# Attention probabilities: dividing on ScalarE and turning by TensorE transposes, in place of one product with a diagonal of 1/sum

## The chip, the cores and the metric

The kernel runs on one core of a Trainium2 chip. The metric is the device time of one execution in microseconds (us), as the median of a few runs. A core has TensorE (PE: matrix products; its weight loads are listed apart as PEld), VectorE (DVE), ScalarE (ACT), GpSimd (POOL) and SyncE (SP, which issues the transfers here). They run side by side and wait for each other by semaphores. TensorE reads from on-chip memory and writes into eight accumulation banks, which the other engines empty.

## The reference, cut to what matters

A decoder trunk of two layers on 512 positions of width 1024. A layer is a feed-forward block, a mixing block and a second feed-forward block, each behind an RMS norm that is modulated by a vector c. The mixing block runs a causal pooling mixer beside latent attention with four heads. In the attention, for each block of 128 queries:

```python
s = (q_nope @ k_nope.T + q_rope @ k_rope.T) * SOFTMAX_SCALE
s = where(qpos >= kpos, s, -inf)
p = softmax(s, axis=-1)      # exp(s - max) / sum
o = p @ v
```

All is in 32-bit floats. The change touches the division by the sum and the way from p (queries on the 128 partitions) to its transpose (keys on the partitions), which the product with v needs.

## The kernel before, in words

Weights come from memory in blocks of up to 128x1024. For each, ScalarE rounds a copy (`hi`, L313) and VectorE takes the rest (`lo`, L316); a product is then three products of rounded values (`mm3`, L324): hi with hi, lo with hi, hi with lo. The values between the stages are split in the same way when they leave their bank (`split_ps`, L507). A product whose operands are plain 32-bit floats is two pairs of weight load and matmul in the trace.

Every instruction is written out in Python in program order, and the framework sorts them into the queues of the engines. A running sum `clock` (L256) books a duration for every product, and functions put off by `later` run at the next `tick` after their booked time; in the attention these are squares and statistics for the norm of the block that follows.

The attention of a layer is eight jobs (L1017): two halves of the queries, four heads each. Job 0 to 3 belong to the first half (query blocks 0 and 1, with 128 and 256 keys), job 4 to 7 to the second (blocks 2 and 3, with 384 and 512 keys). Three functions work on a job:

- `scores`, L1021: per query block the score products and a mask product into one bank (`os`), the negated row maximum on VectorE (L1039, L1040), and one ScalarE instruction that writes exp and leaves its row sum in `sm` (L1042). After both blocks VectorE takes 1/sum (L1046), and builds `dg`, two 128x128 diagonals with 1/sum on them (L1048, `sdg` in the trace).
- `transposes`, L1052: for each pair of a query block and a key block the product of that 128x128 piece of exp with the diagonal of its query block. The piece is the weight, the diagonal streams past it, and the result is turned and divided at once. There are three such products in a job of the first half and seven in one of the second: 40 a layer, 80 in all. Three or four lie side by side in a bank (`t` in the trace), which is then split into `pth` and `ptl`.
- `values`, L1079: the products with v (`opv`), split into `yh` and `yl`.

The loop at L1108 issues the scores of job i, then the transposes of job i-2, then the values of job i-3. Between them stand query projections for heads 2 and 3 (`nope`) and, from step 7 on, output products of the first half (`out_a`, `oo` in the trace). After the last job come the output products of the second half, and then the first products of the feed-forward block (`fg`).

The exp of a job lies in a buffer of the tag `raw`, five of which are shared with the weights that arrive. `dg` has two buffers of its own.

Of the kernel before, what the change touches and what calls it, by code (L numbers as in the profile page):

```python
# [11 lines left out]
F32 = mybir.dt.float32  # L12
# [3 lines left out]
AF = mybir.ActivationFunctionType  # L16
ALU = mybir.AluOpType
AX = mybir.AxisListType

P = 128  # L20
# [62 lines left out]
def trunk(ctx: ExitStack, tc: tile.TileContext, xT, c, pos, vec, cst, ada, wgu, wd, wmix, out):  # L83
    nc = tc.nc
    V, A, G, T = nc.vector, nc.scalar, nc.gpsimd, nc.tensor
# [5 lines left out]
    tmp = ctx.enter_context(tc.tile_pool(name="tmp", bufs=2))  # L91
# [5 lines left out]
    def nm(s):  # L97
        uid[0] += 1
        return f"{s}_{uid[0]}"

    def bank(s="b"):
        return ps.tile([P, S], F32, tag="bank", name=nm(s))
# [35 lines left out]
    ident = const.tile([P, P], F32, name="ident")  # L138
# [117 lines left out]
    clock = [0.0]  # L256
# [5 lines left out]
    def tick():  # L262
        while hooks:
            h = min(hooks, key=lambda e: e[:2])
            if h[0] > clock[0]:
                return
            hooks.remove(h)
            h[2]()

    def mm(o, w, m, start, stop):  # L270
        n = m.shape[-1]
        per = 4 if w.dtype == F32 or (w.dtype == F32R and n < 256) else 1
        clock[0] += per * (n / 2400.0) + 0.0136
        T.matmul(o, w, m, start=start, stop=stop)  # L274
# [30 lines left out]
    def prep(upto, lo_eng=None):  # L305
        while nxt[0] <= min(upto, len(units) - 1):
            key, src, w = units[nxt[0]]
            if nxt[0] not in loaded:
                load(nxt[0])
            raw = loaded.pop(nxt[0])  # L310
            hi = wp.tile([P, 1024], F32R, tag="hi", name=nm("hi"), bufs=NW)
            lo = wp.tile([P, 1024], F32R, tag="lo", name=nm("lo"), bufs=NW)
            A.activation(hi[:, :w], raw[:, :w], AF.Copy)  # L313
            pool = key[0] == "m" and key[2] in POOL_LO
            eng = lo_eng or (G if pool else V)
            eng.tensor_tensor(lo[:, :w], raw[:, :w], hi[:, :w].bitcast(F32), op=ALU.subtract)  # L316
            split[key] = (hi, lo)
            nxt[0] += 1

    def weights(key, ahead=AHEAD):  # L320
        prep(order[key] + ahead)
        return split.pop(key)

    def mm3(blocks, before_hi=None, before_lo=None):  # L324


        n = len(blocks)
        for k, items in enumerate(blocks):
            if before_hi:
                before_hi(k)  # L330
            for o, wh, wl, ah, al in items:
                mm(o, wh, ah, k == 0, False)
            for o, wh, wl, ah, al in items:
                mm(o, wl, ah, False, False)
            tick()
        for k, items in enumerate(blocks):
            if before_lo:
                before_lo(k)
            for o, wh, wl, ah, al in items:
                mm(o, wh, al, False, k == n - 1)  # L340
            tick()
# [165 lines left out]
    def split_ps(o, ts=slice(0, S), sc=None, into=None):  # L507

        hi, lo = into if into is not None else (atile("sh"), atile("sl"))
        if sc is None:  # L510
            A.activation(hi[:, ts], o, AF.Copy)
            V.tensor_tensor(lo[:, ts], o, hi[:, ts].bitcast(F32), op=ALU.subtract)
        else:
            A.activation(hi[:, ts], o, AF.Copy, scale=sc)
            V.scalar_tensor_tensor(lo[:, ts], o, sc, hi[:, ts].bitcast(F32), op0=ALU.mult, op1=ALU.subtract)
        return hi, lo
# [103 lines left out]
    def ffn(l, s, nrm, n_first, steps, end):  # L620
        f = 2 * l + (s == 2)
        c0 = 0
        for h, nf in enumerate(PARTS):
# [24 lines left out]
            if h == 0:  # L648
                keys = [("gu", f, cc, j) for cc in range(n_first) for j in range(2)]
                if isinstance(nrm, Opening):  # L650
                    keys.append(("gu", f, n_first, 0))
                    for ts, os_ in nrm.products(keys):
                        for cc in range(n_first):
                            evac(cc, os_[2 * cc], os_[2 * cc + 1], ts)
                        w = weights(("gu", f, n_first, 1))
                        ou = bank("ou")
                        mm3([[(ou, w[0][:, k * P:(k + 1) * P], w[1][:, k * P:(k + 1) * P], nrm.hh[k], nrm.hl[k])]
                             for k in range(KD)])
                        evac(n_first, os_[-1], ou, ts)
                    n_first += 1  # L660
                else:
                    sc = {}
                    ws = [weights(k, 0) for k in keys]
                    prep(order[keys[-1]] + 4)
                    for ts, os_ in nrm.products(ws):
                        for cc in range(n_first):
                            for o, key in zip(os_[2 * cc:2 * cc + 2], keys[2 * cc:2 * cc + 2]):
                                if ts.start == 0:
                                    sc[key] = nrm.shift(o)
                            evac_first(cc, nrm, os_[2 * cc:2 * cc + 2], [sc[k] for k in keys[2 * cc:2 * cc + 2]], ts)  # L670
                done = n_first
# [149 lines left out]
    def mixer(l, nrm, end):  # L821
# [111 lines left out]
        for h in range(NH):  # L933
            o = bank("okn")
# [22 lines left out]
        for t in range(4):  # L957
            o = bank("ov")
# [10 lines left out]
        for u in range(2):  # L969
            o = bank("oqr")  # L970
# [47 lines left out]
        probs, pts = {}, {}  # L1018
        ya = [(atile("yh"), atile("yl")) for _ in range(0)]

        def scores(job):  # L1021
            half, h = job
            p = wp.tile([P, 1024], F32, tag="raw", name=nm("p"), bufs=NRAW)
            sm = small.tile([P, 2], F32, name=nm("sm"), tag="sm", bufs=4)
            parts = []
            c = 0
            for i in (2 * half, 2 * half + 1):
                n = (i + 1) * P
                nn = max(n, 256)
                qs = slice(i * P, (i + 1) * P)  # L1030
                o = bank("os")
                mm(o[:, :nn], qh[h][0][:, qs], kn[h][0][:, :nn], True, False)
                mm(o[:, :nn], qh[h][1][:, qs], kn[h][0][:, :nn], False, False)
                mm(o[:, :nn], qh[h][0][:, qs], kn[h][1][:, :nn], False, False)
                mm(o[:, :nn], qr[h][:, qs], krh[:, :nn], False, False)
                mm(o[:, :nn], qr[h][:, qs], krl[:, :nn], False, False)
                mm(o[:, qs], identb, negb, False, True)
                m = small.tile([P, 1], F32, name=nm("m"), tag="m", bufs=6)
                V.tensor_reduce(m, o[:, :n], axis=AX.X, op=ALU.max, negate=True)  # L1039
                V.tensor_tensor(m, m, qsc[:, i:i + 1], op=ALU.mult)  # L1040
                pp = p[:, c:c + n]
                A.activation(pp, o[:, :n], AF.Exp, bias=m, scale=qsc[:, i:i + 1], accum_out=sm[:, i % 2:i % 2 + 1])  # L1042
                parts.append(pp)
                c += n
                tick()
            V.reciprocal(sm, sm)  # L1046
            dg = tmp.tile([P, 2, P], F32, name=nm("sdg"), tag="xa", bufs=2)
            V.tensor_tensor(dg, ident.unsqueeze(1).to_broadcast([P, 2, P]),  # L1048
                            sm.unsqueeze(2).to_broadcast([P, 2, P]), op=ALU.mult)
            probs[job] = parts, dg  # L1050

        def transposes(job):  # L1052
            half, h = job
            parts, dg = probs.pop(job)
            hi = wp.tile([P, 1024], F32R, tag="hi", name=nm("pth"), bufs=NW)
            lo = wp.tile([P, 1024], F32R, tag="lo", name=nm("ptl"), bufs=NW)
            for z in (hi, lo):
                G.memset(z[:, 0:P].bitcast(F32), 0.0)
            nj = 2 * half + 2
            last = nj - 1  # L1060
            b0 = bank("t0")

            def tr(dst, i, j):
                mm(dst, parts[i][:, j * P:(j + 1) * P], dg[:, i, :], True, True)

            tr(b0[:, P:2 * P], 1, last)
            tr(b0[:, 2 * P:3 * P], 0, 0)
            tr(b0[:, 3 * P:], 1, 0)
            split_ps(b0[:, P:], slice(P, 512), into=(hi, lo))
            if half:  # L1070
                b1 = bank("t1")
                for j in (1, 2):
                    for i in range(2):
                        tr(b1[:, ((j - 1) * 2 + i) * P:((j - 1) * 2 + i + 1) * P], i, j)
                split_ps(b1, slice(512, 1024), into=(hi, lo))
            tick()
            pts[job] = (hi, lo)
# [142 lines left out]
```

## Time and profile before

| | |
|---|---|
| median of 3 runs | 1812.14 us (1811.38 to 1812.93) |
| the profiled execution | 1813.12 us |
| its span, first to last instruction | 1811.3 us |
| TensorE busy | 1794.9 us, 99% of the span |
| VectorE busy | 1029.7 us, 57% |
| ScalarE busy | 607.2 us, 34% |
| GpSimd busy | 105.2 us, 6% |

The profiled execution is 1.0 us above the median, and 1.8 us of it lie outside the span. The attention stands twice in the span, at about 490 to 536 us and at about 1380 to 1423 us. Successive matmuls overlap in the trace, so the duration of one is longer than what it adds to the chain; what it adds is read from the chain of waits, which follows the work that ended last and gives each piece only its own stretch.

### The profile page before, as it was taken

The numbers are of one execution on the slowest core, as the hardware profiler recorded it, in microseconds if no ns is written. First come the engines' busy times: TensorE is split into PE (matmuls) and PEld (weight loads), VectorE is DVE, ScalarE is ACT, GpSimd is POOL, SyncE is SP. The second block draws the span as 40 slices with busy tenths as digits, with TensorE's granted clock in tenths as the row PEclk, the third lists the DMA queues.
The fourth block names the chain that finished last, engine by engine and source line by source line (L and its number), as shares of the span: only waits on it lengthen the run. The fifth ranks groups of instructions, "written<-read, shape, count | busy, mean of one in ns | idle before, by whom it ended". The sixth has DMA issues, their size and how long they took to land.

```text
span 1811.3 us, 21867 instructions
## 1 busy us (share of the span) xinstructions
PE 1794.9 (99%) x8623; PEld 1505.3 (83%) x8623; DVE 1029.7 (57%) x1591; ACT 607.2 (34%) x906; POOL 105.2 (6%) x206
## 2 busy tenths in 40 slices
PE   7999999999999999999999999999999999999998
PEld 4888888888898888888888888888888988888888
DVE  8675645577878544534676555445787754333333
ACT  3322222344465222223342222223554632221232
POOL 2000000105000000000001000000141000000002
PEclk9999999999999999999999999999999999999999
DMA  8566635633133544534436455443220323233311
GB/s 306 191 220 209 204 126 194 197 100 96 36 100 105 168 147 155 163 118 139 159 111 220 162 196 198 140 139 117 62 88 24 105 82 128 84 104 104 94 47 47
DMA packets 69594, 243.75 MB, mean 135 GB/s; under 512 B 7794, under 2 KB 8946, under 8 KB 69492
## 3 DMA queue, kind: packets, MB, share of 16 engines
q1 hardware_dynamic: 69056, 241.99, 40.8%
q8 instruction: 67, 1.10, 0.3%
q10 hardware_dynamic: 436, 0.38, 0.1%
q14 instruction: 35, 0.29, 0.1%
HBM read 240.24 MB, written 2.10 MB: 134 GB/s over the span
## 4 chain that ended last, share of the span: by engine, by line
PE 98%; DVE 1%; issue 0%; DMA 0%; ACT 0%; POOL 0%; DVEq 0%; ACTq 0%
PE od L274 27%; PE ou L274 25%; PE og L274 24%; PE fg L274 5%; PE oo L274 5%; PE oz L274 5%; PE os L274 2%; PE t L274 1%; PE opv L274 1%; PE oqn L274 1%; PE ov L274 1%; PE okn L274 1%; PE st L274 0%; PE oqr L274 0%; PE rb L274 0%; PE warm L565 0%
## 5 line engine op out<-in xcount | busy, mean ns | idle before, releaser
L313 ACT ACTIVATE hi<-raw 128x1024 fp32r<-128x1024 f32 (+1 forms) x320 | 325.5, 1029 | 377.9 <-PE od L274 211.4
L316 DVE TENSOR_TENSOR lo<-raw,hi 128x1024 fp32r<-128x1024 f32 (+1 forms) x310 | 365.0, 1193 | 52.5 <-ACT hi L313 52.1
L633 DVE TENSOR_TENSOR sg<-sg,ou 128x512 f32<-128x512 f32 x82 | 56.4, 688 | 451.7 <-ACT sg L632 451.7
L274 PE MATMUL od<-gh,hi 128*128 128x512 f32 (+1 forms) x736 | 277.3, 380 | 0.0
L274 PE MATMUL od<-gh,lo 128*128 128x512 f32 (+1 forms) x736 | 277.2, 380 | 0.0
L274 PE MATMUL ou<-hh,hi 128*128 128x512 f32 x656 | 255.2, 389 | 0.0
L274 PE MATMUL ou<-hh,lo 128*128 128x512 f32 x656 | 255.2, 389 | 0.0
L274 PE MATMUL og<-hh,hi 128*128 128x512 f32 x648 | 252.1, 389 | 0.0
L274 PE MATMUL og<-hh,lo 128*128 128x512 f32 x648 | 252.1, 389 | 0.0
L632 ACT ACTIVATE sg<-og 128x512 f32<-128x512 f32 x81 | 48.4, 598 | 607.0 <-PE og L274 607.0
L274 PE MATMUL og<-al,hi 128*128 128x512 f32 x504 | 196.1, 389 | 0.0
L274 PE MATMUL ou<-al,hi 128*128 128x512 f32 x504 | 196.1, 389 | 0.0
L202 DVE SCALAR_TENSOR_TENSOR junk<-ada,c_sb 128x1024 bf16<-128x1024 f32 x144 | 175.3, 1220 | 12.4 <-DMA ada<-in_ada 12.4
L274 PE MATMUL od<-gl,hi 128*128 128x512 f32 (+1 forms) x736 | 176.4, 380 | 0.0
L274 PEld LDWEIGHTS od<-gh,hi 128*128 128x128 f32 x736 | 138.4, 188 | 27.8 <-ACT gh L634 1.2
L693 DVE SCALAR_TENSOR_TENSOR x<-od,mod,x 128x512 f32<-128x512 f32 (+1 forms) x100 | 72.9, 729 | 154.3 <-PE od L274 153.9
L274 PEld LDWEIGHTS od<-gh,lo 128*128 128x128 f32 x736 | 138.4, 188 | 25.9
L274 PEld LDWEIGHTS od<-gl,hi 128*128 128x128 f32 x736 | 134.4, 188 | 26.4
L274 PEld LDWEIGHTS ou<-hh,lo 128*128 128x128 f32 x656 | 123.1, 188 | 25.6
L274 PEld LDWEIGHTS ou<-hh,hi 128*128 128x128 f32 x656 | 123.1, 188 | 25.4
L274 PEld LDWEIGHTS og<-hh,lo 128*128 128x128 f32 x648 | 121.6, 188 | 25.3
L274 PEld LDWEIGHTS og<-hh,hi 128*128 128x128 f32 x648 | 121.6, 188 | 25.2
(249 smaller groups left out, 2318.5 us busy)
## 6 DMA issues: line engine op xcount, KB each, us to landing
raw<-in_wgu SPq DMA_DIRECT2D x176, 512.0 KB, 3.5
ada<-in_ada SPq DMA_DIRECT2D x144, 512.0 KB, 4.4
raw<-in_wd SPq DMA_DIRECT2D x64, 512.0 KB, 4.0
raw<-in_wmix SPq DMA_DIRECT2D x40, 512.0 KB, 3.4
raw<-in_wd SPq DMA_DIRECT2D x32, 384.0 KB, 3.4
raw<-in_wmix SPq DMA_DIRECT2D x6, 384.0 KB, 3.6
x<-in_xT SPq DMA_DIRECT2D x4, 512.0 KB, 5.1
out<-fo SPq DMA_DIRECT2D x7, 256.0 KB, 2.2
```

The lines of the kernel that those rows point to most:

```text
L202: V.scalar_tensor_tensor(junk, w, 1.0, c_sb, op0=ALU.mult, op1=ALU.mult, accum_out=dst)
L274: T.matmul(o, w, m, start=start, stop=stop)
L313: A.activation(hi[:, :w], raw[:, :w], AF.Copy)
L316: eng.tensor_tensor(lo[:, :w], raw[:, :w], hi[:, :w].bitcast(F32), op=ALU.subtract)
L632: A.activation(sg, og, AF.Silu)
L633: V.tensor_tensor(sg, sg, ou, op=ALU.mult)
L693: V.scalar_tensor_tensor(x[d][:, ts], o, gt[:, d:d + 1], x[d][:, ts], op0=ALU.mult, op1=ALU.add)
```

## The change

VectorE no longer builds the diagonals. ScalarE multiplies each of the two blocks of exp by its column of 1/sum, in place, with one copy instruction per block (two a job, 128 and 256 columns wide in the first half, 384 and 512 in the second). The 80 products with a diagonal become 80 transposes of TensorE with the identity, and the running clock books 0.113 us for each, where it booked 4 x 128 / 2400 + 0.0136 = 0.227 us.

```diff
+    def turn(o, m):
+
+        clock[0] += 0.113
+        T.transpose(o, m, ident)
...
             V.reciprocal(sm, sm)
-            dg = tmp.tile([P, 2, P], F32, name=nm("sdg"), tag="xa", bufs=2)
-            V.tensor_tensor(dg, ident.unsqueeze(1).to_broadcast([P, 2, P]),
-                            sm.unsqueeze(2).to_broadcast([P, 2, P]), op=ALU.mult)
-            probs[job] = parts, dg
+            for i, pp in enumerate(parts):
+                A.activation(pp, pp, AF.Copy, scale=sm[:, i:i + 1])
+            probs[job] = parts
 
         def transposes(job):
             half, h = job
-            parts, dg = probs.pop(job)
+            parts = probs.pop(job)
...
             def tr(dst, i, j):
-                mm(dst, parts[i][:, j * P:(j + 1) * P], dg[:, i, :], True, True)
+                turn(dst, parts[i][:, j * P:(j + 1) * P])
```

## Rows read from the trace of the kernel before

**Rows 1.** The page: busy times, TensorE's granted clock in 40 slices, chain by engine.

```profile
PE 1794.9 (99%) x8623; PEld 1505.3 (83%) x8623; DVE 1029.7 (57%) x1591; ACT 607.2 (34%) x906; POOL 105.2 (6%) x206
...
PEclk9999999999999999999999999999999999999999
...
PE 98%; DVE 1%; issue 0%; DMA 0%; ACT 0%; POOL 0%; DVEq 0%; ACTq 0%
```

**Rows 2.** Chain of waits by line, 485 to 550 us, then 1385 to 1440 us.

```profile
by line: PE oo L274 39.6%; PE os L274 22.2%; PE t L274 14.2%; PE opv L274 13.4%; PE oqn L274 10.8%; issue 0.1%
...
by line: PE oo L274 41.9%; PE os L274 19.3%; PE t L274 16.7%; PE opv L274 15.9%; PE fg L274 6.3%; issue 0.1%
```

**Rows 3.** Chain of waits in order of time, first layer: start, length, what.

```profile
497.43 1.38 PE os L274 x12
498.81 0.72 PE t L274 x6
...
505.30 0.72 PE opv L274 x6
...
511.91 1.62 PE t L274 x14
...
516.47 4.36 PE oo L274 x36
520.83 1.56 PE t L274 x14
...
531.15 1.56 PE t L274 x14
532.71 3.00 PE opv L274 x24
```

**Rows 4.** Groups of instructions: the products with the diagonal, and its making.

```profile
L274 PE MATMUL t<-sdg,p 128*128 128x128 f32 x160 | 21.3, 278 | 0.0
...
L274 PEld LDWEIGHTS t<-sdg,p 128*128 128x128 f32 x160 | 19.5, 192 | 0.0
...
L1048 DVE TENSOR_TENSOR sdg<-ident,sm 128x256 f32<-128x256 f32 x16 | 6.7, 420 | 0.5
```

**Rows 5.** Chain of waits elsewhere: one-column products, and the turns at the end.

```profile
415.04 0.79 PE st L274 x8
...
1800.42 1.79 PE tr L274 x16
```

**Rows 6.** Groups of instructions: ScalarE copies with a factor per partition.

```profile
L514 ACT ACTIVATE yph<-op,vec_sb 128x512 fp32r<-128x512 f32 x8 | 5.5, 726 | 0.0
...
L749 ACT ACTIVATE fo<-x,vec_sb 128x256 f32<-128x256 f32 x8 | 3.4, 497 | 0.0
```

**Rows 7.** Stretches of 8 us: length, then busy time of PE, PEld, DVE, ACT, POOL.

```profile
496.00:504.00 8.00, 8.00 (x59) 7.27 (x58) 6.17 (x20) 5.02 (x16) 1.31 (x8) 1.00 0.01 2
504.00:512.00 8.00, 8.00 (x54) 6.62 (x53) 6.17 (x20) 4.36 (x12) 2.33 (x11) 1.00 0.19 66
512.00:520.00 8.00, 8.00 (x63) 7.44 (x62) 5.80 (x15) 5.17 (x14) 1.27 (x8) 1.00 0.20 66
```

**Rows 8.** Timeline of ScalarE in the first layer's attention.

```profile
497.47 0.60 ACT L511 ACTIVATE qh<-oqn 128x512 fp32r<-128x512 f32 x1 [0.38 <-PE oqn L274]
...
506.37 0.78 ACT L1042 ACTIVATE p<-os,m,qsc 128x512 f32<-128x512 f32 x1
507.03 0.21 ACT L1042 ACTIVATION_READ_ACCUMULATOR p<-os,m,qsc 128x1 f32 x1
...
533.26 0.58 ACT L511 ACTIVATE pth<-t 128x512 fp32r<-128x512 f32 x1
```

**Rows 9.** Timeline of VectorE in the first layer's attention.

```profile
507.48 0.15 DVE L1046 RECIPROCAL sm<-sm 128x2 f32<-128x2 f32 x1
...
522.84 0.42 DVE L1048 TENSOR_TENSOR sdg<-ident,sm 128x256 f32<-128x256 f32 x1
...
533.87 0.69 DVE L512 TENSOR_TENSOR ptl<-t,pth 128x512 fp32r<-128x512 f32 x1
```

## The prediction

> **What bounds the kernel now.** I read the page first. TensorE is busy for 99% of the span and holds 98% of the chain that ended last; every slice shows a granted clock of 0.9 or more, the upper level of 2.4 GHz [rows 1]. So time is won or lost only where TensorE's own stretch shrinks or where something makes it wait. Next came the chain cut to the two attention stretches: all of it is TensorE, "issue" is 0.1%, and the products with the diagonal (tile t) hold 14.2% of 65 us in the first layer and 16.7% of 55 us in the second [rows 2]. That is 9.2 us a layer, 18.4 us in all, and over 80 products 0.230 us each. The chain in order of time agrees: 0.72 us for the three of an early job, 1.56 to 1.62 us for the seven of a late one [rows 3]. The group of these products has 160 pairs, so each is two pairs of weight load and matmul [rows 4]. Last I read ScalarE and VectorE in the same stretch, because the change moves work between them: both have room, ScalarE is busy 4.4 to 5.2 of 8 us [rows 7].
>
> **The change part by part.**
>
> *The diagonals* (16 x 0.42 = 6.7 us of VectorE [rows 4]) go. VectorE is not on the chain there, so this is worth nothing by itself; the cover is TensorE at 8.00 of 8 us in each of these stretches [rows 7]. One thing gets earlier: the diagonal of job 7 is made at 522.84, once job 5's buffer is free; its job was ready some 4 us sooner. It was not late for its use at 531.15 [rows 3, 9], so nothing is won.
>
> *The 80 transposes.* No transpose of this kind stands in the trace. The nearest rows from above: half of the present product, one pair that streams the diagonal, costs 1.56 / 14 = 0.111 to 0.72 / 6 = 0.120 us [rows 3]; the turns at the end of the kernel, also two pairs each with 32-bit operands, cost 1.79 / 16 = 0.112 a pair [rows 5]. From below, if a transpose is one pair: products with a single streamed column are the weight load alone, 0.79 / 8 = 0.099 us for the same 128x128 of 32-bit values [rows 5]. And the mask product, one pass of 128 narrow columns with a narrow weight, costs (1.38 - 10 x 0.12) / 2 = 0.09 us, with 0.12 for each of the ten 256-column products, as in opv [rows 3]. These lie close together. I take 0.107 us, between the load alone (0.099) and half of the present product (0.115), since the weight is the same piece of exp and has to be loaded at least once. Then 80 x (0.230 - 0.107) = 9.8 us leave TensorE's stretch; with 0.115 it is 9.2, with 0.099 it is 10.5. The other bound is that it stays two pairs: 0.
>
> *The 16 + 16 copies on ScalarE.* A copy with a factor per partition takes 0.497 us for 256 columns and 0.726 for 512 [rows 6]; by their slope about 0.38 for 128 and 0.61 for 384. A first-half job gets 0.88 us, a second-half job 1.34 us, a layer 8.9 us. ScalarE works in order, and the copies wait for 1/sum: the second exp's sum is read by 507.24 and the reciprocal ends at 507.63 [rows 8, 9], so up to 0.4 us of standing still unless another instruction is put between. Queued behind the copies are the next jobs' exp, pth, yh and the query splits qh. From 496 to 520 us ScalarE is busy 5.02 + 4.36 + 5.17 = 14.6 of 24 us [rows 7]. Added are jobs 1 to 7, 3 x 0.88 + 4 x 1.34 = 8.0 us, and seven waits of some 0.2 us: about 24.0 us. TensorE's own work there loses 19 transposes x 0.123 = 2.3 us, so 21.7 us. ScalarE is then short by up to 2.3 us by the last scores, less if neighbouring instructions overlap as they do now. What hides this is the lag of two steps in the loop: job 4's exp is complete at 507.24 and its turn starts at 511.91, 4.7 us later; behind the last scores stand 4.36 us of oo and then no exp at all [rows 3, 8]. If that cover were gone, 2.3 us a layer would show.
>
> Two places have less cover. At the head, qh of head 3 starts at 497.47 [rows 8] just after job 1's exp, and the scores that need it follow at once on the early turns; copies put ahead of it cost up to 1 us. At the tail, values of job 7 follow the last turn with only values of job 6 between: the turn ends 0.86 us earlier, while the second eviction (pth at 533.26, ptl to 534.56 [rows 8, 9]) may not move, and the 24 products there already take 3.00 us where 24 x 0.12 = 2.88 would do [rows 3]. That gives back 0 to 0.9 us. I take 0.3 us for the head and 0.4 for the tail in each layer: 1.4 us. The range of this term is 0 to 3.5 us.
>
> *The clock of the planner* books 40 x 0.114 = 4.6 us less a layer. It only shifts where squares and statistics are written between the products; their distance to what they wait for stays the same. Nothing. No transfer is added or moved past another, and the exp buffers come free with the turns, sooner than before. Nothing either.
>
> *Sum:* 9.8 - 1.4 = 8.4 us. The profiled execution would go from 1813.1 to 1804.7 us (span 1802.9), and the median, 1.0 us below it, from 1812.1 to **1803.7 us**.
>
> **The rivals.**
>
> *Two pairs remain.* If 32-bit data is turned in two passes, as the present product works, TensorE saves nothing and the copies stay hidden behind an unshortened stretch: 1811.5 to 1813 us. For it: every plain 32-bit product in the trace comes in two pairs [rows 4, 5]. Against: that is how two factors are multiplied, and a transpose multiplies nothing. 0.10.
>
> *A turn does not overlap with its neighbours.* Now each matmul is recorded with 278 ns but adds only 111 to 120 [rows 3, 4], since the next starts before it ends. If transposes could not overlap, each would cost 0.278 us, 80 x (0.278 - 0.230) = 3.8 us more: 1815.9. It decides from 0.230 us upwards; if only the first and last of a job's run stood clear, 32 x 0.16 = 5.1 us of the gain would go. For it: no row shows one. Against: matmuls with different operand types follow each other without such a gap (the mask product's 0.09). 0.04. The Trainium skill ("TensorE: Matmul & The Clock Gate", Part 4: PE-mode transpose) speaks for this side: it gives about 275 ns for a transpose inside a kernel, as an estimate 80 x 0.045 = 3.6 us more, and says that such transposes don't count as busy for the clock. The trace has 278 ns for products that cost 111 to 120, so a duration of that size need not be a price.
>
> *ScalarE paces the attention.* Place: 496 to 520 us of the first layer and its like in the second. If the scores wait for banks that exp frees late, all the copies and waits show, 8.9 + 8 x 0.2 = 10.5 us a layer at most, 21 - 9.8 = 11 us slower, 1823. It ends slower than before once 4.9 us a layer show; by the sum above 2.3 us are there to show. 0.04 for slower; 0.07 for a part of it, 3 to 8 us given back in all and 1806.5 to 1810.
>
> *A turn is cheaper still.* A product of 256 columns costs 0.12 us with its load hidden [rows 3], so 128 columns with a hidden load would be 0.06: 80 x 0.17 = 13.6 us, 1798.5 to 1800. Against it: 0.099 for the load alone. 0.03. The Trainium skill ("TensorE: Matmul & The Clock Gate", Terms) calls the transpose mode four times faster for 32-bit data; by that the estimate is 0.230 / 4 = 0.058 us and a gain of 13.8 us. No row here shows it.
>
> **How the numbers follow.** The forecast has 0.72, with its own range from 9.2 - 3.5 to 10.5 us, 1801.7 to 1806.5. The rivals hold 0.10, 0.04, 0.04 + 0.07 and 0.03. A measurement of this kernel tells a difference of about 0.2% (3.6 us) from none. Faster by more: 0.72 + 0.03 + 0.05 of the part-paced case = 0.80. Within it: 0.10 + 0.02 = 0.12. Slower: 0.08. The range from 1800.0 to 1811.0 takes in the forecast, the part-paced case and the cheaper edge of two pairs.
>
> **What would show it.** One load and one matmul per turn, 80 instead of 160, and pieces of t in the chain of about 0.33 us and 0.75 us instead of 0.72 and 1.56. TensorE at 8.00 of 8 us throughout the attention, with ScalarE near 7 of 8 between 496 and 520. The clock still at the upper level. The forecast is wrong if t keeps two pairs, if the chain shows ScalarE (L1042, L511 or the new copies) before os, opv or t, or if the last values wait for ptl by more than 1 us a layer.

## The result, and the profile after

| | before | after |
|---|---|---|
| median | 1812.41 us (4 runs, 1811.38 to 1812.93) | 1802.83 us (4 runs, 1802.53 to 1803.62) |
| ratio | | 0.9945 (0.9933 to 0.9958) |
| profiled execution | 1813.12 us | 1803.62 us |
| its span | 1811.3 us | 1801.8 us |
| TensorE busy | 1794.9 us | 1786.1 us |
| VectorE busy | 1029.7 us | 1023.2 us |
| ScalarE busy | 607.2 us | 621.1 us |

The change makes the kernel 9.6 us faster, 0.55%. The forecast was 1803.7 us, with 1801.7 to 1806.5 as its own range. The page of the changed kernel, in the lines that answer to [rows 1]:

```profile
PE 1786.1 (99%) x8543; PEld 1496.0 (83%) x8543; DVE 1023.2 (57%) x1575; ACT 621.1 (34%) x938; POOL 103.2 (6%) x206
...
PEclk9999999999999999999999999999999999999999
...
PE 98%; DVE 0%; DMA 0%; ACT 0%; issue 0%; DVEq 0%; ACTq 0%; SPq 0%
```

TensorE still holds the chain, at the same clock, with 80 matmuls fewer. The chain by line, 485 to 550 us and 1375 to 1440 us, where [rows 2] had 14.2% of 65 us and 16.7% of 55 us for t:

```profile
by line: PE oo L274 39.6%; PE os L274 22.2%; PE opv L274 13.6%; PE oqn L274 12.1%; PE t L327 6.8%; PE fg L274 5.9%; issue 0.1%
...
by line: PE oo L274 35.4%; PE os L274 20.1%; PE fg L274 16.2%; PE opv L274 13.6%; PE t L327 6.8%; PE oqn L274 5.8%; PE rb L274 1.4%; PE st L274 1.2%; issue 0.1%
```

That is 4.4 us in each layer, where 9.2 stood. In order of time, against [rows 3]:

```profile
491.18 1.38 PE os L274 x12
...
498.21 1.38 PE os L274 x12
499.59 0.33 PE t L327 x3
...
511.12 0.77 PE t L327 x7
511.89 0.72 PE opv L274 x6
...
514.84 4.36 PE oo L274 x36
...
527.92 0.76 PE t L327 x7
528.68 3.11 PE opv L274 x24
...
533.14 13.04 PE oo L274 x85
```

Three turns take 0.33 us instead of 0.72, seven take 0.76 or 0.77 instead of 1.56 or 1.62: 0.11 us each, one pair. What stands around them (os 1.38, oo 4.36, opv 0.72) kept its length; only the last values grew, from 3.00 to 3.11 us. The ends of the attention in the chain of the kernel before:

```profile
490.40 1.38 PE os L274 x12
...
537.06 13.05 PE oo L274 x85
```

From the first score product to the output products of the second half the attention took 46.66 us before (490.40 to 537.06) and 41.96 after (491.18 to 533.14); the second layer gives the same two lengths (1376.87 to 1423.53, 1372.93 to 1414.89). 2 x 4.70 = 9.4 us is the whole result but for 0.1 to 0.2 us.

That the spans agree so closely with this is partly chance. In the traced executions the attention begins 0.78 us later after the change, because the opening took longer, and the span ends 0.9 us sooner behind the last eviction (4.3 us behind it, where it was 5.2). Both vary between executions: over the traces of all runs the first score product starts between 488.6 and 491.2 us. The length of the attention, the same to 0.06 us in both layers of a run where the clock stays up, is the sharper measure, and it is given below beside the medians.

The groups of instructions, against [rows 4]; L1053 are the new copies:

```profile
L1053 ACT ACTIVATE p<-p,sm 128x128 f32<-128x128 f32 (+3 forms) x32 | 16.2, 554 | 0.9 <-DVE sm L1051 0.9
...
L327 PE MATMUL t<-ident,p 128*128 128x128 f32 x80 | 11.4, 273 | 0.0
...
L327 PEld LDWEIGHTS t<-ident,p 128*128 128x128 f32 x80 | 8.7, 140 | 0.0
```

And the stretches of 8 us, against [rows 7] (fourth busy column ScalarE):

```profile
496.00:504.00 8.00, 8.00 (x57) 7.14 (x56) 6.45 (x19) 7.20 (x21) 1.41 (x8) 1.00 0.00 0
504.00:512.00 8.00, 8.00 (x56) 6.62 (x55) 5.94 (x18) 7.71 (x20) 2.07 (x12) 1.00 0.21 68
512.00:520.00 8.00, 8.00 (x63) 7.44 (x62) 5.69 (x16) 7.89 (x20) 1.03 (x6) 1.00 0.21 66
```

ScalarE went from 14.6 to 22.8 of 24 us, and TensorE lost nothing by it: 8.00 of 8 us in each, and no wait of ScalarE in the chain of the attention.

### The profile page after: what moved, and what is told of

It is laid out like the page before. It is cut to its first block, busy times and chain, and to the rows that moved or that the text cites. A ratio compares the mean times of both kernels' runs of the same rounds, so it can differ in the third digit from the quotient of the medians.

```text
span 1801.8 us, 21711 instructions
## 1 busy us (share of the span) xinstructions
PE 1786.1 (99%) x8543; PEld 1496.0 (83%) x8543; DVE 1023.2 (57%) x1575; ACT 621.1 (34%) x938; POOL 103.2 (6%) x206
## 4 chain that ended last, share of the span: by engine, by line
PE 98%; DVE 0%; DMA 0%; ACT 0%; issue 0%; DVEq 0%; ACTq 0%; SPq 0%
PE od L274 27%; PE ou L274 25%; PE og L274 24%; PE fg L274 5%; PE oo L274 5%; PE oz L274 5%; PE os L274 2%; PE opv L274 1%; PE oqn L274 1%; PE ov L274 1%; PE okn L274 1%; PE t L327 0%; PE st L274 0%; PE oqr L274 0%; PE rb L274 0%; PE warm L570 0%
## 5 line engine op out<-in xcount | busy, mean ns | idle before, releaser
L274 PEld LDWEIGHTS ou<-hh,lo 128*128 128x128 f32 x656 | 123.2, 188 | 25.6
```

## The experiments

All are edits of the changed kernel. Differences are between medians where nothing else is said, ratios are to the kernel before, measured beside each experiment. Its median was 1812.2 to 1813.0 us there, so differences of less than 1 us say little. Two kinds of question are asked: which part of the change the 9.6 us come from and what its cover (the work of TensorE behind which the copies stay hidden) was worth, and what sets the price of a turn.

**The product back, the division left on ScalarE.**

```diff
-                turn(dst, parts[i][:, j * P:(j + 1) * P])
+                mm(dst, parts[i][:, j * P:(j + 1) * P], ident, True, True)
```

> The division stays on ScalarE, but each of the 80 pieces is turned by a plain 32-bit product with the identity (two pairs of weight load and matmul) instead of a transpose. Theory (the gain is TensorE's: a turn is one pair at 0.11 us where the product with the diagonal took two, and the copies on ScalarE are hidden): 80 x 0.12 = 9.6 us come back, ratio to before 1.000 within 0.1%, t in the chain again 0.72 us for three and 1.56 for seven. Rival (part of the gain comes from VectorE's lost diagonals and the freed buffers): 2 to 5 us faster than before remain, ratio 0.997 to 0.999. Rival (the copies cost something that the gain hid): 1 to 4 us slower than before.

1812.33 us, ratio 0.9995 (0.9987 to 1.0004). The whole gain goes away. The chain in this run:

```profile
499.39 0.72 PE t L274 x6
...
512.50 1.62 PE t L274 x14
```

These are the pieces of [rows 3] to the hundredth, and the attention takes 46.68 us where it took 46.66. So moving the division, with VectorE's diagonals gone and 32 copies more on ScalarE, is worth nothing either way, and the gain is that of the transposes alone. Both rivals fall by the chain; by the ratio alone the edge of the first (0.9987 to 0.999) would still be open.

**No division at all.**

```diff
-            for i, pp in enumerate(parts):
-                A.activation(pp, pp, AF.Copy, scale=sm[:, i:i + 1])
```

> The changed kernel without the 32 copies on ScalarE: the division of the probabilities by their sum is left out, the transposes stay. Theory: TensorE's chain is the same and the copies were hidden, so the time is that of the changed kernel within 0.5 us, ratio to before 0.994 to 0.995. Rival (the copies give back 1.4 us or more, as the prediction put it): 1.4 us or more below the changed kernel, ratio 0.9937 or less.

1802.3 us, ratio 0.9939 (0.9926 to 0.9951), 0.5 us below the changed kernel. The ratio stands at the edge between the two expectations and its interval takes in both. The chain decides:

```profile
490.05 1.38 PE os L274 x12
...
527.55 3.11 PE opv L274 x24
...
532.01 13.04 PE oo L274 x85
```

The attention takes 41.96 us, as long as with the copies, in both layers. So the copies cost nothing there. The 3.11 us of the last values also stand here, without any copy: they belong to the shorter turns.

**Every copy twice.**

```diff
+            for pp in parts:
+                A.activation(pp, pp, AF.Copy, scale=ones[:, 0:1])
```

> The changed kernel with every copy followed by a second one of the same size (by 1.0): 8 us more of ScalarE a layer, in a stretch of 24 us where the changed kernel shows ScalarE busy for 22.8. Theory (the copies are hidden, but with little to spare): ScalarE's queue falls some 5 us behind by the last scores, the lag of two steps covers about half, and 2 to 4 us a layer show: 4 to 8 us above the changed kernel, ratio 0.9967 to 0.999, with ScalarE's exp or pth as what TensorE waits for. Rival (the cover is wide): less than 1 us above it. Rival (the changed kernel is already paced by ScalarE): the full 13 to 16 us, ratio 1.002 or more.

1809.53 us, ratio 0.9982 (0.9973 to 0.999): 6.7 us above the changed kernel, 3.4 a layer, inside the expected 2 to 4. (By the attention it is 3.3 and 3.4: 45.26 and 45.32 us.) One stretch of 8 us, parts of the chain in order of time, and the waits of TensorE's matmuls in the first layer's attention (us in total, times, longest):

```profile
512.00:520.00 8.00, 6.40 (x44) 5.46 (x45) 4.03 (x10) 8.00 (x19) 1.03 (x6) 1.00 0.21 66
...
511.98 1.23 ACT p L1053 x2
...
514.60 1.41 ACT p L1047 x4
...
516.38 1.12 ACT p L1053 x2
517.50 1.11 ACT p L1055 x2
518.62 0.48 ACT pth L516
...
PE oo L274 <- ACT yh L516: 1.6, 1, 1.6
PE opv L274 <- ACT pth L516: 0.6, 1, 0.6
```

From 512 to 519.4 us the chain is ScalarE's, and TensorE stands for 1.6 of 8 us. This is the rival of the prediction that ScalarE paces the attention, in part and at the place that was named. But the longest wait is that of the output products for yh, the rounded values, which stand behind the copies in ScalarE's queue; expected were exp or pth. One set of copies fits under the lag of two steps, two do not.

**The division on VectorE.**

```diff
-                A.activation(pp, pp, AF.Copy, scale=sm[:, i:i + 1])
+                V.tensor_scalar(pp, pp, sm[:, i:i + 1], None, op0=ALU.mult)
```

> The changed kernel with the division by VectorE in place of ScalarE. Theory (where the division runs does not matter while TensorE is fed): the time of the changed kernel within 0.7 us, ratio 0.994 to 0.9955, ScalarE back at 4 to 5 of 8 us and VectorE near 7 of 8. Rival (VectorE, with the maxima, the low parts and the sums in its queue, is the tighter one): 2 us or more above the changed kernel.

1802.84 us, ratio 0.9944 (0.993 to 0.9958): no difference that the medians can show. VectorE shows 7.68 of 8 us from 504 to 512, ScalarE 6.29, more than the expected 4 to 5. The chain shows a small cost: the attention takes 42.29 and 42.30 us instead of 41.96, 0.3 us a layer. Here the first two products of job 0's values follow directly on the turns of job 1, ahead of most of job 3's scores, and their weight load waits:

```profile
PEld opv L274 <- ACT pth L516: 0.3, 1, 0.3
```

Whether this order comes from the place of the division or would change with another small edit was not tried.

**The old booking.**

```diff
-        clock[0] += 0.113
+        clock[0] += 0.227
```

> The changed kernel with 0.227 us booked for a turn, as for the product before; nothing else differs, only the places at which squares and statistics are written move by up to 4.6 booked us a layer. Theory (the booking is worth nothing here): the time of the changed kernel within 0.7 us, ratio 0.994 to 0.9955. Rival (the shorter booking lets later work be put better or worse): 2 us or more of difference.

1802.13 us, ratio 0.994 (0.9927 to 0.9954). No difference that can be measured; the attention takes the same 41.96 us.

**Every turn twice.**

```diff
                 turn(dst, parts[i][:, j * P:(j + 1) * P])
+                turn(dst, parts[i][:, j * P:(j + 1) * P])
```

> The changed kernel with every transpose issued twice into the same place: 80 further turns and nothing else on any engine. Theory (a turn adds 0.11 us to TensorE's chain wherever it stands): 80 x 0.11 = 8.8 us above the changed kernel, ratio 0.9985 to 1.000. Rival (a turn costs more at its neighbours' borders than inside a row of turns, so that the first of a row bears a part): less than 7 us above it.

1811.45 us, ratio 0.9991 (0.9982 to 1.0): 8.6 us above the changed kernel. Two of its pieces in the chain:

```profile
499.33 0.66 PE t L327 x6
...
512.18 1.53 PE t L327 x14
```

0.11 us for each added turn, in long rows and in short ones: the attention takes 46.25 us, 4.29 more for 40 turns. Three turns cost 0.33 and six 0.66, so a first turn costs no more than the next, and no cost shows at the border with other products.

**A second turn with half the weight columns.**

```diff
+                T.transpose(dst[0:64], parts[i][:, j * P:j * P + 64], ident)
```

> The changed kernel with a second transpose behind each, of the first 64 columns of the same piece only: half the weight columns are loaded, the same 128 columns of the identity stream. Theory (the load of 128 columns of 32 bits is what a turn costs, the pass hides behind it): 0.05 to 0.07 us for each, 4 to 5.6 us above the changed kernel. Rival (the stream of 128 columns of 32 bits sets the price): 0.11 us each, 8.8 us above it.

1810.78 us, ratio 0.999 (0.9981 to 0.9999): 8.0 us above the changed kernel, 0.10 us for each. The attention takes 46.24 us, as with every turn twice (46.25): 0.11 us for each. The group of added products and that of their loads (L1069 is the added turn):

```profile
L1069 PE MATMUL t<-ident,p 128*64 128x128 f32 x80 | 18.3, 272 | 0.0
...
L1069 PEld LDWEIGHTS t<-ident,p 128*64 128x64 f32 x80 | 8.9, 111 | 0.0
```

The load got shorter (111 ns where the full turn's has 141), the price did not. My theory that the load sets it falls. The stream of 128 columns is left, and a price fixed per turn; the next experiments are to tell these apart.

**A second turn with half the streamed columns, and one with half of both.** These leave out half of the partitions of the piece, so that only 64 columns of the identity stream.

```diff
+                T.transpose(dst[:, 0:64], parts[i][0:64, j * P:(j + 1) * P], ident[0:64, 0:64])
```

> The changed kernel with a second transpose behind each, of the upper 64 of the 128 partitions of the same piece: 128 weight columns are loaded as in a full turn, but only 64 columns of the identity stream. A second turn with 64 loaded and 128 streamed columns cost 0.11 us, as much as a full one. If the stream alone sets the price: 0.05 to 0.06 us each, 4 to 5 us above the changed kernel. If load and stream are two equal bounds that overlap (one-column products cost 0.099 us for the load alone): 0.10 us each, 8 us above it. If the price is fixed per turn: 0.11 us, 8.8 us above it.

```diff
+                T.transpose(dst[0:64, 0:64], parts[i][0:64, j * P:j * P + 64], ident[0:64, 0:64])
```

> The changed kernel with a second transpose behind each, of a 64x64 corner of the same piece: half the columns loaded, half streamed. If load and stream are two equal bounds, each in proportion to its columns: 0.05 to 0.06 us each, 4 to 5 us above the changed kernel. If the price is fixed per turn: 0.10 to 0.11 us, 8 to 9 us above it.

1834.17 us, ratio 1.012 (1.0105 to 1.0135), and 1830.0 us, ratio 1.0096 (1.008 to 1.0113): 31.3 and 27.2 us above the changed kernel. None of the expectations held: something else came in. The timeline of TensorE in the first of the two, and two stretches of 8 us (the third number from the end is the granted clock):

```profile
515.75 0.33 PE L327 MATMUL t<-ident,p 128*128 128x128 f32 x1
516.01 0.27 PE L1069 MATMUL t<-ident,p 64*128 64x64 f32 x1
516.21 0.33 PE L327 MATMUL t<-ident,p 128*128 128x128 f32 x1
...
512.00:520.00 8.00, 8.00 (x42) 5.96 (x42) 4.09 (x11) 6.11 (x14) 1.45 (x8) 0.95 0.24 76
520.00:528.00 8.00, 8.00 (x50) 6.90 (x49) 3.99 (x11) 4.87 (x12) 0.70 (x4) 0.84 0.15 55
```

From full turn to full turn it is 516.21 - 515.75 = 0.46 us, where two full turns take 0.22. Each matmul here starts when the one before is nearly over, instead of 0.11 us after it. 80 x (0.46 - 0.11) = 28 us. The rest is the clock: after rows of such alternating turns it falls from 2.4 to 1.2 GHz for a part of the stretch, 0.95 and 0.84 on average here and 0.79 from 1424 to 1432 us; (0.05 + 0.16 + 0.21) x 8 = 3.4 us. The sum is 31.4 for 31.3 measured. In the other kernel the pair takes 0.43 us, and the same sum with its stretches (0.99 and 0.80, second layer undisturbed) gives 25.6 + 1.7 = 27.3 for 27.2. There the two layers price the clock by themselves: the attention takes 56.55 us in the disturbed one and 55.06 in the other, 1.5 us apart. The clock fell behind 3 of the 16 rows of seven such pairs in the two kernels, each time about 0.6 us after the row; such a row takes some 3 us in which TensorE does nothing but turns.

**The half turns in rows.** To part the change of the partition count from the price of a half turn, a bank's half turns stand together behind its full ones.

```diff
+            def half_turns():
+                for dst, i, j in again:
+                    T.transpose(dst[:, 0:64], parts[i][0:64, j * P:(j + 1) * P], ident[0:64, 0:64])
+                again.clear()
...
+            half_turns()
             split_ps(b0[:, P:], slice(P, 512), into=(hi, lo))
```

> The second turns of the upper 64 partitions again (128 columns loaded, 64 streamed), but all of a bank's together behind its full turns instead of one behind each: two changes between 128 and 64 partitions for a bank, 48 in all, where there were 160. If the 0.24 us that an alternating pair cost beyond two full turns lies at the change of the partition count (the load of the next piece no longer under the pass of the one before): the half turns inside a row cost 0.05 to 0.11 us each and each change about 0.12 us, 80 x 0.05 to 0.11 + 48 x 0.12 = 10 to 15 us above the changed kernel, 1813 to 1818 us. If every turn of 64 partitions stands by itself: 80 x 0.2 us or more inside the rows too, 1822 us or more. Inside a row: 0.055 us if the stream sets the price, 0.10 if the load of 128 columns is an equal bound.

1814.56 us, ratio 1.0009 (0.9999 to 1.0019): 11.7 us above the changed kernel, inside the expected 10 to 15. The chain of a late job (L1071 are the half turns):

```profile
527.94 0.33 PE t L327 x3
528.26 0.33 PE t L1071 x3
528.59 0.59 PE t L327 x4
529.18 0.39 PE t L1071 x4
```

The fourth half turn in a row adds 0.39 - 0.33 = 0.06 us: half the streamed columns, about half the price, with 128 columns loaded (137 ns for a load, 140 for that of a full turn). So the price is neither fixed per turn nor set by the loaded columns. The stream is what is left; but a half turn halves the partitions along with the streamed columns, and no run parts these two. The four full turns that follow half turns take 0.59 us where 4 x 0.11 = 0.44 would do: a change of the partition count costs some 0.15 us. 80 x 0.06 + 48 x 0.15 = 12 us, for 11.7 by the medians and 12.1 by the attention (48.03 us). The same two prices give the alternating pair: 0.11 + 0.06 + 2 x 0.15 = 0.47 for 0.46. The clock stays at 1.00.

**More turns by transposes.** Two other kinds of plain product with the identity in this kernel, as transposes.

```diff
 def rms_rows(y, nb):
...
-            mm(rb[:, i * P:(i + 1) * P], y[:, i:i + 1].to_broadcast([P, P]), ident, True, True)
+            turn(rb[:, i * P:(i + 1) * P], y[:, i:i + 1].to_broadcast([P, P]))
...
-                    mm(o[i][d // 4][:, d % 4 * P:d % 4 * P + P], self.xg[d // 2][:, c:c + P], ident, True, True)
+                    T.transpose(o[i][d // 4][:, d % 4 * P:d % 4 * P + P], self.xg[d // 2][:, c:c + P], ident)
```

> The changed kernel with two further kinds of product with the identity done by transposes: the 16 turns of the output's second half at the end of the kernel (tile tr) and the 34 that spread a row of norm factors over the partitions (tile rb). Theory (each such product is two pairs on TensorE's chain and becomes one): 50 x 0.11 = 5.5 us below the changed kernel, about 1797.3 us, ratio 0.9915. Rival (the turns at the end stand beside work that waits anyway, and those of rb in the chain of the norm): 2 to 4 us.

1798.13 us, ratio 0.9921 (0.9909 to 0.9934): 4.7 us below the changed kernel by the medians, 3.7 by the spans of the profiled executions (1801.8 and 1798.1). The chain at a norm, and at the end of the kernel:

```profile
420.80 0.44 PE rb L327 x4
...
1781.09 6.98 PE od L274 x58
...
1788.09 0.49 DVE x L698
...
1788.67 0.42 ACT sq L401
...
1789.12 0.44 DVE acc L402
...
1789.69 0.59 PE st L274 x4
```

Four factors take 0.44 us instead of 0.89. The chain holds 30 of the 34 after the opening, in eight places: 30 x 0.11 = 3.3 us for rb. The 16 turns at the end gave nothing. In the changed kernel they filled 1.79 us between the last od and st [rows 5 has the same piece], and st took 0.44; now the chain runs through VectorE and ScalarE from 1788.06 to 1789.69, 1.63 us, which the turns had covered, and st takes 0.59: 2.22 us for 2.23. So the theory holds for rb and the rival for the turns at the end, and the chain's 3.3 us lie in the rival's 2 to 4. What the spans and medians show beyond that is in no piece of the chain behind the opening.

## Why the prediction was right, point by point

**What bounds the kernel.** TensorE before and after, 98% of the chain; 9.4 of the 9.6 us lie in its stretch of the attention. Shown by both chains, and by the experiments without the division and with the old booking, which touch other engines and leave the attention at 41.96 us.

**The price of a turn.** 0.107 us was taken, 0.110 came (4.4 us for 40 in the chain). One pair, 80 instead of 160, as forecast. The term was 9.8 us, and the traces give 18.4 - 8.8 = 9.6. The reason given for the number was half wrong: I leaned on the load of the piece (0.099 for the one-column products), and the experiments speak against the load and leave the stream of 128 columns. That the two prices are nearly equal here is luck; by it the sum did not suffer. What the 0.099 us of a one-column product consist of stays open: a half turn loads 128 columns too, of 64 partitions, and costs 0.06.

**What is given back at head and tail.** This term was mis-sized: 1.4 us was taken, some 0.2 came. At the tail the last values take 3.11 instead of 3.00 us, 0.1 a layer, where 0.4 was taken; the mechanism named there, turns that end earlier while the eviction does not, fits the kernel without copies, which shows the same 3.11. At the head, 0.3 was taken for copies that might come ahead of qh of head 3; the order of ScalarE in the changed kernel shows why nothing came of it:

```profile
498.25 0.60 ACT L516 ACTIVATE qh<-oqn 128x512 fp32r<-128x512 f32 x1 [0.23 <-PE oqn L274]
498.84 0.80 ACT L1053 ACTIVATE p<-p,sm 128x128 f32<-128x128 f32 x2
499.96 0.49 ACT L516 ACTIVATE pth<-t 128x384 fp32r<-128x384 f32 x1 [0.32 <-PE t L327]
```

qh goes first, the copies of job 1 after it, and they are done before the turns of job 1 at 501.31. With both terms together the gain was forecast 1.2 us too small (8.4 for 9.6); the median of the kernel before, 0.3 us higher in the result than in the forecast, left the time 0.9 us below the forecast. (The bounds of the forecast's own range, from 1812.1 us, should read 1801.6 and 1806.4.)

**ScalarE's load.** For 496 to 520 us 14.6 + 8.0 = 22.6 us of work were forecast, and 22.8 came. The seven waits of 0.2 us, which made 24.0 of it, can't be checked by busy time. The cover was named as the lag of two steps. With one set of copies it was whole, as the kernel without copies shows; a second set is no longer hidden and costs 3.4 us a layer.

**Diagonals, buffers and booking at nothing:** shown, by the product put back (ratio 0.9995, attention 46.68 for 46.66 us) and by the old booking (41.96 us).

**The rivals.** Two pairs: excluded, 80 loads and matmuls stand in the trace. No overlap with the neighbours: excluded for these turns, since doubling them adds 0.11 us each. The Trainium skill's page for this side ("TensorE: Matmul & The Clock Gate", Part 4: PE-mode transpose) gives about 275 ns for a transpose in a kernel, beside a figure for bf16; the group here, of 32-bit values, has 273 ns, and it is a duration and not a price. That such transposes don't count as busy for the clock, as the same section of the Trainium skill says, is neither shown nor excluded here: the granted clock stays at 1.00 through the rows of turns in the changed kernel, 0.77 us at most; it fell only in the two kernels with alternating pairs, where turns alone fill some 3 us. ScalarE as the pace: excluded for one set of copies, since without any the attention is as long. A cheaper turn: excluded at 0.11, though the reason given against it, the load, did not hold. The four times that the Trainium skill gives ("TensorE: Matmul & The Clock Gate", Terms) would be 0.058; the turn came out 0.230 / 0.110 = 2.1 times cheaper.

## What to carry to other kernels

A 32-bit product with the identity or a diagonal that stands on TensorE's chain is worth a transpose: half the price here, 0.11 for 0.23 us, and what the diagonal did besides can go to an engine that has room. Price the cover before such a move: add the moved work to that engine's busy time in the very stretch, and look how many steps lie between its result and the use; here 22.8 of 24 us were still free of cost, and one more set of copies was not. Where products fill the time of a wait for other engines, as the turns at the end of this kernel did, making them cheaper gives nothing back.

## What the runs showed of the hardware that was not expected

A turn's price followed the columns that stream, or the partitions, which were halved with them (0.11 us for 128, 0.06 for 64 inside a row), and not the weight columns (64 instead of 128: 0.11 by the chain). A change between turns of 128 and of 64 partitions broke the overlap of neighbouring products, some 0.15 us each time; with a change at every turn a pair took 0.46 instead of 0.22 us. In that kernel TensorE was busy for 8.00 of 8 us, and yet the granted clock fell to a mean of 0.84 in one stretch; with the same turns sorted into rows it stayed at 1.00. Alternating also made a row of turns about twice as long (3.1 us for seven pairs, where the sorted ones take 1.6 and the doubled full turns 1.5). Whether the broken overlap or the longer time with turns alone brings the fall about was not tried.
